# Sums of squares on TensorE, and a first pair's products with the memory's k tiles between them, in a hybrid decoder step

## The chip, the cores and the metric

One core of one Trainium2 chip runs the whole program. The metric is the time of one execution on the device in microseconds (us); the time before is the median of three runs. One further execution was recorded by the profiler; all durations of single instructions are from that one. The engines are TensorE (PE, with its weight loads as PEld), VectorE (DVE), ScalarE (ACT), GpSimd (POOL) and SyncE (SP), whose queue issues all the loads and stores. Every engine takes its own instructions strictly in the order that was fixed when the program was built.

## What is computed

One layer of a decoder step over 1,024 prompt tokens and 8 x 4 sample tokens, model width 2,048, in fp32. Cut to what matters here:

```python
def mixer_layer(x, mem_k, mem_v, ...):
    hn = rmsnorm(x, g_norm)
    proj = hn @ w_in                     # 5904 columns, split among the groups
    ...                                  # A: gated short conv, B: GLA, C: sliding window
    q = rmsnorm(m_q.reshape(b, L, MEM_HEADS, MEM_HD), g_mem_q)
    s = jnp.einsum('blhd,bmhd->bhlm', q, mem_k) * (MEM_HD ** -0.5)
    o_mem = jnp.einsum('bhlm,bmhd->blhd', jax.nn.softmax(s, axis=-1), mem_v)
    ...
    return x + mix @ w_out

def memory_kv(mem, g_mem, w_mem_kv, g_mem_k):        # 256 memory tokens
    kv = rmsnorm(mem, g_mem) @ w_mem_kv              # 2048 x 1024
    k, v = jnp.split(kv, 2, axis=-1)
    return rmsnorm(k.reshape(b, m, MEM_HEADS, MEM_HD), g_mem_k), v.reshape(...)
```

## The kernel before

Features lie on the 128 partitions, the 1,056 tokens (1,024 + 32) along the free axis; `H` is half of them (528), `CG` a quarter (264), `CW` a third (352). A k tile is 128 of the 2,048 features, so there are 16. An fp32 product is made of three TensorE passes: each operand is split into a rounded part h (cast by ACT) and the rest l (subtraction by DVE), and hh, lh and hl are added.

The program runs in stages:

1. **First two** (`first_two`, L380 to L417). Two projection tiles, Dq0 and Dq1, are computed from all 16 k tiles of x times the gain, without the row norm, while x is loaded (`load_x`, L274). ACT squares each k tile (L289) and DVE adds the squares up (L294). At the end `row_norms` (L321) sums over the features on TensorE, forms the reciprocal roots on DVE in small steps (L261 to L270), spreads them over the partitions by transposes (L337) and copies them to `R` (L340, L342). Six evacuations (L417) multiply the two tiles by R. The first 8 k tiles of x stay in SBUF as four blocks B11, B12, B21, B22 (`x0raw`, tiles `xb`).
2. **Memory** (`memory`, L814). 16 k tiles of memory tokens against `w_mem`: 32 weight pieces of 128 x 512, two per k tile, 6 matmuls each (L865). A piece is loaded (`load_piece`, L349), cast by ACT (L364) and subtracted by DVE (L368); odd pieces go to tiles named t, even ones to wh and wl. Between the k tiles runs the generator `first_strands`, which prepares the token operands of the next stage: it normalises the blocks in place (L443), takes a low-rank gate product of them (`rank`, L485), combines the blocks (L458, L459, L464, L473) and splits the seven operands (L431 on ACT, L432 on DVE). What is left of the generator runs after the last k tile.
3. **Pairs** (`first_pair`, L670). 24 pairs of projection tiles; each pair multiplies its weights with the 2 x 2 blocks of x by seven products, in the order B11, T2, B21, T1, T3, B22, T4, 24 matmuls each (`product`, L635, matmuls at L650). This is done for the first 8 k tiles and, by `second_pair`, for the other 8, and then again for the output projection. It is the bulk of the run. Beside each half product one step of a queue of generators (`pipe`) runs: here `memory_out` and the cross-attention heads `d_head`.

Memory pieces and the pairs' weight pieces come from one pool of six buffers, `wr`. A pair has four pieces, (0,0), (1,0), (1,1) and (0,1); those of the first pair are requested ahead of the memory, and `make_weights`, called by `product`, makes the seven weight sets of a pair one by one and requests the next pair's pieces:

```python
wr = self.wp.tile([P, 512], F32, name=self.name("wr"), tag="wr", bufs=6)     # load_piece
t = self.wp.tile([P, 512], F32, name=self.name("wr"), tag="wr", bufs=6)      # load_weights
...
if i == 0:                                                                   # make_weights
    self.load_weights(n + 1, ((0, 0), (1, 0)))
    x = r(0, 0)
elif i == 1:
    v.tensor_tensor(s1, r(1, 0), r(1, 1), op=ALU.add)
    v.tensor_tensor(s2, s1, r(0, 0), op=ALU.subtract)
...
elif i == 4:
    x = r(1, 0)
    v.tensor_tensor(x, r(0, 0), x, op=ALU.subtract)
```

A buffer is free for the next request when the last instruction that reads its piece is done: for a memory piece that is the subtraction at L368; for (0,0) of a pair the difference of set 4, which may be taken early; for (1,0), (0,1) and (1,1) the sets 4, 5 and 6, that is the fifth, sixth and seventh product.

Of the kernel before, what the change touches and what calls it, by code (L numbers as in the profile page):

```python
# [14 lines left out]
P = 128  # L15
# [107 lines left out]
class _Step:  # L123
# [149 lines left out]
    def load_x(self):  # L273
# [3 lines left out]
        self.acc = [None] * 2  # L277
# [8 lines left out]
        def square(k, parts):  # L286
# [33 lines left out]

    def row_norms(self, spare):  # L321

        nc = self.nc
        acc = self.acc[0]
        nc.vector.tensor_tensor(acc, acc, self.acc[1], op=ALU.add)
        for sums in self.token_sums(acc[:, 0:SEQ]):
            pass
        nc.tensor.matmul(spare[:, 0:2], acc[:, TOK - P : TOK], self.ones[:, 0:2], start=True,
                         stop=True)
        r = self.small(NB + 1, tag="rx")  # L330
        self.rsqrt(r[:, 0:NB], sums, 1.0 / D_MODEL, EPS, NB)
        self.rsqrt(r[:, NB : NB + 1], spare[:, 0:1], 1.0 / D_MODEL, EPS, 1)
        for g in range(3):
            ps = self.ps() if g == 1 else spare
            blocks = list(range(4 * g, min(4 * g + 4, NB + 1)))
            for i, n in enumerate(blocks):
                nc.tensor.transpose(ps[:, i * P : i * P + P],  # L337
                                    r[:, n : n + 1].to_broadcast([P, P]), self.ident)
            if g < 2:
                nc.scalar.copy(self.R[:, 512 * g : 512 * g + 512], ps)  # L340
            else:
                nc.scalar.copy(self.R[:, SEQ:TOK], ps[:, P - NS : P])  # L342
# [43 lines left out]
    def first_two(self, evacs):  # L386

        nc = self.nc
        a, b = self.two(), self.two()
# [7 lines left out]
        for kq in range(4):  # L397
            w = [self.take(1) for _ in range(2)]
            for kk in range(4):
# [11 lines left out]
                if kq == 3 and kk == 1:  # L411
                    self.row_norms(b[:, 512:1024])
        for i in range(2):
            dst = evacs[i]
            for c in range(NCH):
                cs = slice(c * CW, c * CW + CW)
                nc.vector.tensor_tensor(dst[:, cs], ps[i][c][:, 0:CW], self.R[:, cs], op=ALU.mult)  # L417

# [15 lines left out]
    def first_strands(self):  # L434
# [5 lines left out]
        for k in range(8):  # L440
            for i in range(2):
# [3 lines left out]
            if k % 2:  # L445
                yield
# [1456 lines left out]
```

## Time and profile before

| | us |
|---|---|
| median of 3 runs | 1579.18 (1578.06 to 1580.34) |
| the profiled execution | 1580.26 |
| its span on the core | 1578.5 |
| PE busy in the span | 1531.3 (97%) |
| DVE busy | 1105.2 (70%) |
| ACT busy | 775.0 (49%) |

The span is from the first to the last instruction; the profiled execution's own time is 1.8 us more. A row of a profile's timeline gives start and duration in us, engine, line, operation, written tile <- read tiles, shapes, count, and in brackets how long the engine had been idle and what ended that. A row of grouped instructions gives, behind the bar, busy time in us and the mean of one in ns, and then the idle time just ahead of them. Matmuls are pipelined: the distance of two starts is what one costs, not the duration shown. Granted clock is the share of full speed that TensorE had.

### The profile page before, as it was taken

What the parts mean: (1) busy time and instruction counts of PE and PEld (TensorE: products, weight loads), DVE (VectorE), ACT (ScalarE), POOL (GpSimd) and SP (SyncE); (2) the same over time, 40 slices, a digit from 0 to 9 for tenths busy, and PEclk for the clock granted to TensorE, in tenths of its full rate; (3) what the DMA queues carried; (4) which work ended last, traced back from release to release, by engine and by line L of the source; (5) the groups of instructions that cost most, each with busy time, mean ns of one, the idle gap of its engine ahead of it and who ended that gap; (6) DMA issues with size and microseconds to landing.
All of it is one profiled execution on the core that took longest, in us unless ns stands there. A gap on an engine that the chain in (4) does not pass through costs nothing.

```text
span 1578.5 us, 30825 instructions
## 1 busy us (share of the span) xinstructions
PE 1531.3 (97%) x12194; PEld 1453.0 (92%) x12194; DVE 1105.2 (70%) x2280; ACT 775.0 (49%) x1622; POOL 23.3 (1%) x35
## 2 busy tenths in 40 slices
PE   8878999999999999999999999999999999999998
PEld 7646999999999999988998888999989999999998
DVE  8998455577555559566767776769779767596664
ACT  8565733222333326563458766445457444263332
POOL 3000000000000000000000000000000000000000
PEclk9999999999999999999999999999999999999999
DMA  7433123266332347358423244245537324587651
GB/s 272 144 107 114 67 101 109 103 244 241 109 108 103 109 144 279 104 126 302 144 84 83 97 88 122 94 134 140 176 111 245 109 96 152 201 285 276 210 204 63
DMA packets 104756, 236.79 MB, mean 150 GB/s; under 512 B 16804, under 2 KB 22820, under 8 KB 104612
## 3 DMA queue, kind: packets, MB, share of 16 engines
q1 hardware_dynamic: 104612, 234.82, 44.7%
q8 instruction: 96, 1.57, 0.4%
q14 instruction: 48, 0.39, 0.1%
HBM read 165.38 MB, written 69.41 MB: 149 GB/s over the span
## 4 chain that ended last, share of the span: by engine, by line
PE 79%; DVE 9%; DMA 5%; ACT 4%; issue 2%; SPq 0%; DVEq 0%; ACTq 0%
PE pj L650 68%; DMA x<-in_xT 2%; DVE wl L632 1%; DMA wr<-in_w_mem 1%; PE ms L865 1%; DVE s L432 1%; PE ms L1224 1%; PE ms L972 1%; PE ms L1002 1%; PE ms L1278 1%; PE ms L1266 1%; DMA sx<-xs 1%; DVE xhl L311 1%; DMA kcd<-in_cache_swa_kT 1%; ACT xhl L310 1%
## 5 line engine op out<-in xcount | busy, mean ns | idle before, releaser
L650 PE MATMUL pj<-s,wh 128*128 128x264 f32 x6720 | 1274.9, 288 | 9.5 <-ACT pj L733 9.0
L650 PEld LDWEIGHTS pj<-s,wh 128*128 128x128 f32 x6720 | 1054.5, 189 | 34.1 <-issue 15.7
L650 PE MATMUL pj<-s,wl 128*128 128x264 f32 x3360 | 957.3, 285 | 0.0
L650 PEld LDWEIGHTS pj<-s,wl 128*128 128x128 f32 x3360 | 634.8, 189 | 3.9 <-issue 3.4
L631 ACT CAST wh<-wr 128x512 fp32r<-128x512 f32 x300 | 186.5, 622 | 252.3 <-PE pj L650 230.6
L632 DVE TENSOR_TENSOR wl<-wr,wh 128x512 fp32r<-128x512 f32 x300 | 206.6, 689 | 112.6 <-ACT wh L631 108.4
L680 DVE TENSOR_TENSOR d<-d,pj 128x528 f32<-128x528 f32 x180 | 121.4, 701 | 112.8 <-PE pj L650 65.6
L631 ACT CAST wh<-ws 128x512 fp32r<-128x512 f32 x120 | 74.5, 621 | 106.8 <-PE pj L650 100.4
L632 DVE TENSOR_TENSOR wl<-ws,wh 128x512 fp32r<-128x512 f32 x120 | 82.7, 689 | 7.0 <-ACT wh L631 6.5
L733 ACT COPY pj<-d 128x528 f32<-128x528 f32 x120 | 72.5, 604 | 16.6 <-DVE u L743 7.3
L432 DVE TENSOR_TENSOR s<-sx,s 128x1056 fp32r<-128x1056 f32 x42 | 51.7, 1254 | 1.8 <-ACT s L431 1.6
L431 ACT CAST s<-sx 128x1056 fp32r<-128x1056 f32 x42 | 44.3, 1079 | 9.9 <-DMA sx<-xs 5.1
L683 ACT COPY d<-pj 128x528 f32<-128x528 f32 x30 | 18.0, 600 | 61.0 <-PE pj L650 61.0
L754 DVE TENSOR_TENSOR d<-d,pj 128x528 f32<-128x528 f32 x30 | 21.1, 704 | 35.7 <-PE pj L650 35.7
L757 DVE TENSOR_TENSOR d<-u,pj 128x528 f32<-128x528 f32 x30 | 21.1, 704 | 34.1 <-PE pj L650 34.0
L689 ACT COPY d<-pj 128x528 f32<-128x528 f32 x30 | 18.0, 601 | 52.2 <-PE pj L650 52.2
L613 DVE TENSOR_TENSOR ws<-wr,wr 128x512 f32<-128x512 f32 x60 | 41.3, 689 | 1.6 <-DMA wr<-in_w_in 0.5
L627 DVE TENSOR_TENSOR wr<-wr,ws 128x512 f32<-128x512 f32 x60 | 41.3, 689 | 1.1
L623 DVE TENSOR_TENSOR wr<-wr,wr 128x512 f32<-128x512 f32 x60 | 41.3, 689 | 1.0
L614 DVE TENSOR_TENSOR ws<-ws,wr 128x512 f32<-128x512 f32 x60 | 41.3, 689 | 1.0
L700 ACT COPY d<-pj 128x528 f32<-128x528 f32 x30 | 18.0, 600 | 47.7 <-PE pj L650 47.7
L696 ACT COPY d<-pj 128x528 f32<-128x528 f32 x30 | 18.0, 600 | 47.1 <-PE pj L650 47.1
(365 smaller groups left out, 1545.2 us busy)
## 6 DMA issues: line engine op xcount, KB each, us to landing
wr<-in_w_in SPq DMA_DIRECT2D x184, 256.0 KB
half_in<-d SPq DMA_DIRECT2D x44, 528.0 KB
d<-half_in SPq DMA_DIRECT2D x44, 528.0 KB
sx<-xs SPq DMA_DIRECT2D x42, 528.0 KB
wr<-in_w_out SPq DMA_DIRECT2D x64, 256.0 KB
x<-in_xT SPq DMA_DIRECT2D x24, 528.0 KB
xs<-t SPq DMA_DIRECT2D x36, 264.0 KB
half_out<-d SPq DMA_DIRECT2D x16, 528.0 KB
```

Source lines behind the costliest of these rows:

```text
L431: nc.scalar.copy(h[:, s], x)
L432: nc.vector.tensor_tensor(l[:, s], x, h[:, s].bitcast(F32), op=ALU.subtract)
L613: v.tensor_tensor(s1, r(1, 0), r(1, 1), op=ALU.add)
L614: v.tensor_tensor(s2, s1, r(0, 0), op=ALU.subtract)
L623: v.tensor_tensor(x, r(0, 0), x, op=ALU.subtract)
L627: v.tensor_tensor(x, x, self.wsum[n][1], op=ALU.subtract)
L631: nc.scalar.copy(wh, x)
L632: v.tensor_tensor(wl, x, wh.bitcast(F32), op=ALU.subtract)
L650: nc.tensor.matmul(ps[:, 512 * c : 512 * c + CG], w[:, ks], x[:, xs], start=(first and kk == 0 and n == 0), stop=(kk == 3 and n == 2), ski ...
L680: nc.vector.tensor_tensor(o, o, bank(ps), op=op)
L733: nc.scalar.copy(bank(ps), x)
L754: tt(ws, zs, bank(w), op=ALU.add)
```

## The change

Three things are changed.

First, the squares. DVE adds nothing; each k tile's squares go to TensorE as they are, in `sum_squares`: four matmuls against a matrix of ones, each 32 columns wide at its own place, accumulate a quarter of the tokens each in a PSUM tile `sums` over all k. Those of the last three k tiles stand behind the main matmuls of k tile 13, and `row_norms` is now a generator whose three parts run beside k tiles 13, 14 and 15. `R` and the two evacuation tiles are requested later.

Second, the order of memory and first pair. `memory` is a generator too, and is not run by itself any more: `product` runs a step of `first_strands` and one k tile of the memory in turn as long as its token operand isn't ready, and `first_strands` runs what is left of the memory ahead of T4. The strands are made in another order, block by block, B11 first. While an operand is missing, `product` makes no weight sets ahead. The masks and the first two heads come behind the first pair.

Third, the memory's tokens are loaded by two transfers of 8 k tiles, and their squares are added in halves.

```diff
@@ load_x @@
-            i = int(k % 4 == 3)
-            if self.acc[i] is None:
-                self.acc[i] = sq
-            else:
-                nc.vector.tensor_tensor(self.acc[i], self.acc[i], sq, op=ALU.add)
+            self.sq[k] = sq
@@ sum_squares, row_norms @@
+    def sum_squares(self, k):
+        for j in range(4):
+            self.nc.tensor.matmul(self.sums[32 * j : 32 * j + 32, 0:CG], self.ones[:, 0:32],
+                                  self.sq[k][:, CG * j : CG * j + CG], start=(k == 0),
+                                  stop=(k == KT - 1), tile_position=(0, 32 * j))
+        self.sq[k] = None
     def row_norms(self, spare):
-        acc = self.acc[0]
-        nc.vector.tensor_tensor(acc, acc, self.acc[1], op=ALU.add)
...
+        rows = self.t5()[:, 0:CG]
+        nc.scalar.copy(rows, self.sums[:, 0:CG])
+        yield
...
+        self.rsqrt(r, t[:, 0:2], 1.0 / D_MODEL, EPS, 8)
+        self.rsqrt(r8[0:8, :], t[0:8, 2], 1.0 / D_MODEL, EPS, 4)
+        yield
+        for j in range(4):
...
+            nc.scalar.copy(self.R[:, CG * j : CG * j + CG], ps[:, 0:CG])
+        yield
@@ first_two @@
-                if kq == 3 and kk == 1:
-                    self.row_norms(b[:, 512:1024])
+                self.sum_squares(k)
+                if k == KT - 3:
+                    for i in (1, 2):
+                        self.sum_squares(k + i)
+                    self.R = self.rtile("R")
+                    norms = self.row_norms(b[:, 512:1024])
+                if k >= KT - 3:
+                    next(norms)
...
@@ first_strands @@
+        normal(0)
+        yield
+        self.split(B11, b11)
+        yield
+        normal(1)
...
+        ranks(range(4))
+        normal(3)
+        yield
+        self.split(B22, b22)
...
+        self.split(T2, b11)
+        yield
+        self.split(B21, b21)
...
+        self.split(T1, b12)
+        yield
+        self.split(T3, b22)
+        yield
+        for _ in self.mem:
+            pass
         self.split(T4, t4)
+        yield
@@ product @@
-        while len(self.wready) <= min(self.wdone + 2, 7 * len(self.pairs) - 1):
+        ahead = 0 if None in self.S else 2
+        while len(self.wready) <= min(self.wdone + ahead, 7 * len(self.pairs) - 1):
             self.make_weights()
+        while self.S[i] is None:
+            next(self.first)
+            next(self.mem, None)
@@ memory @@
             mh, ml = parts[k]
-            next(between, None)
             for c in range(2):
                 wh, wl = self.take(2)
...
-        for _ in between:
-            pass
+            yield
@@ run @@
-                self.memory(pool, self.first_strands())
-                self.masks()
-                for h in range(2):
-                    self.d_head(q[h], h)
+                self.mem, self.first, self.mem_done = self.memory(pool), self.first_strands(), []
                 for n, two in enumerate(self.two_in):
...
                     self.first_pair(self.keep(self.kept(two)))
+                    if n == 0:
+                        self.masks()
+                        for h in range(2):
+                            self.d_head(q[h], h)
```

In the rows below, line numbers of the change are those of the changed file: L636 is the request in `load_weights` (L599 before), L359 that in `load_piece` (L349), L378 the subtraction of a piece (L368), L468 the normalising of a block (L443), L454 the subtraction of a token operand (L432), L691 a product's matmul (L650) and L904 the memory's (L865).

SP's queue at the end of the first stage, before: requests of pieces in the six `wr` buffers, four for the first pair (`in_w_in`), then the memory's third piece and those behind it (`in_w_mem`).

```order
L599 DMA wr86_709<-in_w_in 128x512
L599 DMA wr87_711<-in_w_in 128x512
L599 DMA wr88_713<-in_w_in 128x512
L599 DMA wr89_715<-in_w_in 128x512
L349 DMA wr100_743<-in_w_mem 128x512
L439 DMA t599_737<-in_w_ga 128x256
L349 DMA wr103_749<-in_w_mem 128x512
L349 DMA wr106_761<-in_w_mem 128x512
```

The same place after the change:

```order
L636 DMA wr85_757<-in_w_in 128x512
L636 DMA wr86_759<-in_w_in 128x512
L636 DMA wr87_761<-in_w_in 128x512
L889 DMA mr101_788<-in_memT 128x8x256
L889 DMA mr102_790<-in_memT 128x8x256
L636 DMA wr88_763<-in_w_in 128x512
L636 DMA wr92_768<-in_w_in 128x512
L636 DMA wr93_770<-in_w_in 128x512
L461 DMA t596_776<-in_w_ga 128x256
L359 DMA wr107_804<-in_w_mem 128x512
L359 DMA wr110_810<-in_w_mem 128x512
L359 DMA wr113_822<-in_w_mem 128x512
```

Two pieces of the second pair (wr92 and wr93) now stand between the first pair's four and the memory's third piece, wr107, and the memory's tokens (mr) are ahead of them.

DVE in the memory stage, before: weight subtractions (t and wl from a piece wr) with the normalising of blocks xb between them.

```order
L368 TENSOR_TENSOR wl_817<-wr_789,wh_816 128x512
L368 TENSOR_TENSOR t_829<-wr_814,t_828 128x512
L443 SCALAR_TENSOR_TENSOR xb_130<-xb_130,consts,R_118 128x528
L443 SCALAR_TENSOR_TENSOR xb_132<-xb_132,consts,R_118 128x528
L443 SCALAR_TENSOR_TENSOR xb_130<-xb_130,consts,R_118 128x528
L443 SCALAR_TENSOR_TENSOR xb_132<-xb_132,consts,R_118 128x528
L368 TENSOR_TENSOR wl_845<-wr_826,wh_844 128x512
L837 SCALAR_TENSOR_TENSOR r_867<-mr_801,consts,r_866 128x256 x2
```

After, between two of the early pieces (from the sixth on, wr_838):

```order
L378 TENSOR_TENSOR t_853<-wr_838,t_852 128x512
L468 SCALAR_TENSOR_TENSOR xb_130<-xb_130,consts,R_653 128x528
L454 TENSOR_TENSOR s_975<-xb_129,s_974 128x1056
L468 SCALAR_TENSOR_TENSOR xb_128<-xb_128,consts,R_653 128x528
L454 TENSOR_TENSOR s_975<-xb_130,s_974 128x1056
L378 TENSOR_TENSOR wl_909<-wr_850,wh_908 128x512
L468 SCALAR_TENSOR_TENSOR xb_128<-xb_128,consts,R_653 128x528 x3
L494 TENSOR_TENSOR xb_129<-xb_129,xb_127 128x1056
L494 TENSOR_TENSOR xb_130<-xb_130,xb_127 128x1056
L378 TENSOR_TENSOR t_921<-wr_906,t_920 128x512
```

And after, from the thirteenth piece (wr_998) on:

```order
L378 TENSOR_TENSOR wl_1017<-wr_998,wh_1016 128x512
L378 TENSOR_TENSOR t_1029<-wr_1014,t_1028 128x512
L378 TENSOR_TENSOR wl_1075<-wr_1026,wh_1074 128x512
L378 TENSOR_TENSOR t_1087<-wr_1072,t_1086 128x512
L872 SCALAR_TENSOR_TENSOR r_1128<-mr_790,consts,r_1127 128x256 x2
L378 TENSOR_TENSOR wl_1102<-wr_1084,wh_1101 128x512
L378 TENSOR_TENSOR t_1114<-wr_1099,t_1113 128x512
L378 TENSOR_TENSOR wl_1136<-wr_1111,wh_1135 128x512
```

Early pieces have four to six wide operations on blocks between two weight subtractions, normalising and splitting mixed; from the thirteenth piece on little but the pieces' own subtractions and the memory tokens' (r from mr) is left.

PE at the end of the memory, before: the last piece's matmuls (ms) and then the first product (pj) in one run.

```order
L865 MATMUL ms_720<-t_1240,r_1164 128x512
L865 MATMUL ms_722<-t_1240,r_1164 128x512
L865 MATMUL ms_720<-t_1241,r_1164 128x512
L865 MATMUL ms_720<-t_1240,r_1165 128x512
L865 MATMUL ms_722<-t_1241,r_1164 128x512
L865 MATMUL ms_722<-t_1240,r_1165 128x512
L650 MATMUL pj_1307<-s_976,wl_1314 128x264
L650 MATMUL pj_1307<-s_977,wh_1313 128x264
L650 MATMUL pj_1307<-s_976,wh_1313 128x264
```

After, in the second product, T2 (s_1123 and s_1124 are the two parts of its operand, r_900 and r_901 the two parts of the memory's fifth and sixth k tile):

```order
L904 MATMUL ms_786<-wh_952,r_901 128x512
L691 MATMUL pj_767<-s_1123,wh_891 128x264
L691 MATMUL pj_767<-s_1123,wl_892 128x264
L904 MATMUL ms_785<-t_964,r_900 128x512
L904 MATMUL ms_787<-t_964,r_900 128x512
L904 MATMUL ms_785<-t_965,r_900 128x512
L904 MATMUL ms_785<-t_964,r_901 128x512
L904 MATMUL ms_787<-t_965,r_900 128x512
L904 MATMUL ms_787<-t_964,r_901 128x512
L691 MATMUL pj_767<-s_1124,wh_891 128x264
L691 MATMUL pj_767<-s_1123,wh_891 128x264
L691 MATMUL pj_767<-s_1123,wl_892 128x264
```

The products' matmuls now stand between the memory's, from its third k tile to its last one, and each waits in PE's order for the pieces ahead of it.

More of the change, by code (lines that the diff above doesn't have):

```diff
@@ L326, in row_norms @@
-        for sums in self.token_sums(acc[:, 0:SEQ]):
-            pass
[L328 to L342, printed above, removed]
+        rows = self.t5()[:, 0:CG]
@@ new lines, in row_norms @@
+        nc.scalar.copy(rows, self.sums[:, 0:CG])
+        yield
+        for x in range(2):
+            nc.tensor.transpose(spare[:, x * P : x * P + P], rows[:, x * P : x * P + P],
+                                self.ident)
+        nc.tensor.transpose(spare[0:8, 2 * P : 3 * P], rows[:, 2 * P : CG], self.ident)
+        t = spare[:, 0 : 3 * P].rearrange("p (x j c) -> p x j c", x=3, j=4)[:, :, :, 0]
+        r, r8 = self.small(8, tag="rx"), self.small(4, tag="rx8")
+        self.rsqrt(r, t[:, 0:2], 1.0 / D_MODEL, EPS, 8)
@@ new lines, in row_norms @@
+        self.rsqrt(r8[0:8, :], t[0:8, 2], 1.0 / D_MODEL, EPS, 4)
+        yield
+        for j in range(4):
+            ps = spare if j % 2 else self.sums
+            for x in range(2):
+                nc.tensor.transpose(ps[:, x * P : x * P + P],
+                                    r[:, 4 * x + j : 4 * x + j + 1].to_broadcast([P, P]),
+                                    self.ident)
+            nc.tensor.transpose(ps[:, 2 * P : CG], r8[0:8, j : j + 1].to_broadcast([8, P]),
+                                self.ident[0:8, 0:8])
+            nc.scalar.copy(self.R[:, CG * j : CG * j + CG], ps[:, 0:CG])
@@ L384, in take, with first_two @@
         return self.ready[p]
-    def first_two(self, evacs):
+    def first_two(self):
         nc = self.nc
+        self.sums = self.ps()
         a, b = self.two(), self.two()
@@ L417, in first_two @@
                 nc.vector.tensor_tensor(dst[:, cs], ps[i][c][:, 0:CW], self.R[:, cs], op=ALU.mult)
+        self.sums = None
+        return evacs
     def split(self, i, src, half=None):
@@ L811, in gate, with memory @@
         return lambda *z: self.pipe.now(work(*z))
-    def memory(self, pool, between):
+    def memory(self, pool):
         nc, I, O = self.nc, self.I, self.O
@@ L842, in squares @@
             nonlocal acc
[L843 removed]
+            t = raw[k][:, 0 : 8 * N_MEM]
             nc.scalar.activation(t, t, AF.Square)
[L845 to L851 removed]
+            for w in (4 * N_MEM, 2 * N_MEM, N_MEM):
+                nc.vector.tensor_tensor(t[:, 0:w], t[:, 0:w], t[:, w : 2 * w], op=ALU.add)
+            if k:
+                nc.vector.tensor_tensor(acc, acc, t[:, 0:N_MEM], op=ALU.add)
+            else:
+                acc = self.hp.tile([P, H], F32, name=self.name("acc"), tag="u", bufs=1)[:, 0:N_MEM]
+                nc.vector.tensor_copy(acc, t[:, 0:N_MEM])
+        for k in range(2):
+            raw[k] = self.stile(F32, "mr")
+            nc.sync.dma_start(out=raw[k][:, 0 : 8 * N_MEM].rearrange("p (k t) -> p k t", k=8),
+                              in_=I["memT"][8 * k : 8 * k + 8].rearrange("k p t -> p k t"))
         prepare(0)
@@ L855, in memory @@
                 prepare(k + 2)
-            if k % 4 == 2:
-                squares(k // 4)
+            if k % 8 == 6:
+                squares(k // 8)
+                raw[k // 8] = None
             mh, ml = parts[k]
-            next(between, None)
             for c in range(2):
```

60 lines of the change are left out of this document (21 added, 39 removed).

## The prediction

> **What bounds the kernel now.** I read the page's first part, then busy times by stretch, then the chain of waits where TensorE is not full. Over the whole span TensorE (PE) is the limit; the second fence gives, for six stretches of 20 us, length, busy time of PE, PEld, DVE, ACT and POOL, granted TensorE clock, DMA share and GB/s.
>
> ```profile
> PE 1531.3 (97%) x12194; PEld 1453.0 (92%) x12194; DVE 1105.2 (70%) x2280; ACT 775.0 (49%) x1622; POOL 23.3 (1%) x35
> ```
>
> ```profile
> 60.00:80.00 20.00, 17.21 (x83) 11.60 (x84) 17.83 (x36) 9.04 (x16) 0.00 (x0) 0.91 0.50 159
> 80.00:100.00 20.00, 16.10 (x88) 9.17 (x87) 18.89 (x22) 13.58 (x21) 0.00 (x0) 1.00 0.31 103
> 100.00:120.00 20.00, 14.99 (x51) 9.53 (x50) 19.82 (x23) 14.14 (x18) 0.00 (x0) 0.91 0.36 108
> 120.00:140.00 20.00, 15.62 (x65) 10.66 (x64) 16.12 (x34) 10.55 (x21) 1.05 (x5) 1.00 0.38 124
> 140.00:160.00 20.00, 18.98 (x151) 17.71 (x150) 14.84 (x60) 12.66 (x36) 0.00 (x0) 1.00 0.35 110
> 160.00:180.00 20.00, 20.00 (x146) 18.49 (x145) 12.98 (x38) 14.59 (x39) 0.00 (x0) 1.00 0.19 70
> ```
>
> PE has gaps until about 146 us and none after; between 60 and 140 us VectorE (DVE) is nearly full. So the time is set by how late PE becomes full and by the PE work then left. Two rows of the chain give the point and the price of a product's matmul: 60.94/502 = 0.121 us. The two groups below are the first pair's matmuls that ran before 146 us: 27 + 14 = 41 of 7 x 24 = 168.
>
> ```profile
> 146.06 3.77 PE pj L650 x31
> ...
> 199.08 60.94 PE pj L650 x502
> ```
>
> ```profile
> L650 PE MATMUL pj<-s,wh 128*128 128x264 f32 x27 | 5.1, 287 | 0.0
> L650 PE MATMUL pj<-s,wl 128*128 128x264 f32 x14 | 4.1, 289 | 0.0
> ```
>
> Without the cross-attention heads, which both kernels do beside full products, the second pair would start at 146.06 + 127 x 0.121 = 161.5 us. **That is the mark**: the change wins or loses what its second pair starts earlier or later.
>
> In the memory stage each of 32 weight pieces of `w_mem` is loaded into a buffer `wr`, cast by ScalarE (ACT), subtracted by DVE, and only then is its buffer free for the next load. The chain of waits shows one such turn, and the loads' queue waits for the subtraction (total us, times, longest):
>
> ```profile
> 91.05 2.66 DMA wr<-in_w_mem
> ...
> 93.73 0.63 ACT t L364
> ...
> 94.39 0.69 DVE t L368
> ...
> 104.63 3.32 DMA wr<-in_w_mem
> ...
> 109.35 2.87 DMA wr<-in_w_mem
> ```
>
> ```profile
> SPq L349 <- DVE wl L368: 36.1, 13, 8.2
> ...
> SPq L349 <- DVE t L368: 8.4, 12, 2.3
> ```
>
> A turn without a queue is 2.66 + 0.63 + 0.69 and gaps, 4.05 us. With DVE's queue it was longer: the odd pieces' subtractions run from 72.25 to 137.61 us, 13 turns of 5.03 us.
>
> ```profile
> 72.25 0.69 DVE L368 TENSOR_TENSOR t<-wr,t 128x512 fp32r<-128x512 f32 x1
> ...
> 137.61 0.69 DVE L368 TENSOR_TENSOR t<-wr,t 128x512 fp32r<-128x512 f32 x1
> ```
>
> **The buffers, the part that decides.** There are six `wr` buffers. Before, the first pair's four pieces hold four of them through the whole memory stage, so memory pieces go through the other two, and two turns run side by side: two pieces per 5 us. After, the first pair's first weights are made ahead of most of the memory, and `make_weights` at its first step loads two pieces of the second pair (SP's rows in the section on the change have them ahead of the memory's third piece). Only piece (0, 0) of the first pair has been given back by then: its sums are formed early. So 3 + 2 = 5 buffers are held and **one** is left, until the fifth product's weights (T3, piece (1, 0)) are made. The memory's first two pieces are loaded earlier; the next 22 go through one buffer, one after the other; the last 8 go through two. That is 22 + 4 = 26 turns in series, where before 15 pairs of turns sufficed.
>
> **The first stage.** Removed: DVE's additions of squares and the trailing norms. Added: 16 x 4 fp32 matmuls of 32 columns on PE. The rows give 18 main matmuls in 43.73 - 40.83 = 2.90 us, and four such sums of 256 tokens in 55.64 - 55.08 = 0.56, so 0.58 at 264.
>
> ```profile
> 12.55 0.32 PE L408 MATMUL pj<-xhl,wh 128*128 128x352 f32 x1
> ...
> 40.83 1.62 PE L408 MATMUL ms<-xhl,r 128*128 128x352 f32 x9
> ...
> 43.73 1.62 PE L408 MATMUL ms<-xhl,r 128*128 128x352 f32 x9
> ...
> 55.08 0.64 PE L937 MATMUL ms<-sq,ones 128*32 128x256 f32 x8 [0.24 <-DVE sq L325]
> 55.64 0.38 PE L328 MATMUL pj<-ones,sq 128*128 128x2 f32 x2
> ...
> 63.23 0.32 PE L408 MATMUL pj<-xhl,wh 128*128 128x352 f32 x1
> ```
>
> PE is already the pace there, so the sums are not hidden. Main matmuls end at 12.55 + 15 x 2.90 + 16 x 0.58 = 65.3 us, where the row above has the last three groups from 62.3 to 63.5. Bounds of the sums: nothing, if they fit into PE's small waits, to 16 x 0.64 = 10.2; I take 9.3, the value of the nearest row. The additions saved on DVE give nothing once PE sets the pace. The last three sums stand ahead of the last two k tiles, so the norms' sums and reciprocal roots lie under 36 main matmuls; after them come the spreading of the norms over R, the six evacuations and the first block.
>
> ```profile
> L443 DVE SCALAR_TENSOR_TENSOR xb<-xb,consts,R 128x528 f32<-128x528 f32 x16 | 11.2, 764 | 0.0
> L368 DVE TENSOR_TENSOR t<-wr,t 128x512 fp32r<-128x512 f32 x15 | 10.3, 689 | 0.7 <-ACT t L364 0.5
> ...
> L417 DVE TENSOR_TENSOR dq<-pj,R 128x352 f32<-128x352 f32 x3 | 1.5, 525 | 0.1
> ```
>
> ```profile
> 60.39 0.65 PE L337 MATMUL pj<-ident,sm 128*128 128x128 f32 x4 [1.30 <-DVE sm L270]
> ...
> 61.70 1.01 DVE L417 TENSOR_TENSOR dq<-pj,R 128x352 f32<-128x352 f32 x2
> ```
>
> From 65.3 us: from the norms' transposes to the first evacuation 1.3, as between these two rows; six evacuations at 0.5, 3.0; four normalisings at 11.2/16 = 0.70, 2.8; one weight subtraction 0.7. The fourth memory piece is ready at about **73 us**.
>
> **From 73 us, nine turns paced by DVE.** Between the fourth and the thirteenth subtraction DVE's order holds the normalising, combining and splitting of blocks, from these rows and the two of L443 and L368 above:
>
> ```profile
> L432 DVE TENSOR_TENSOR s<-xb,s 128x2112 fp32r<-128x2112 f32 x4 | 9.3, 2352 | 0.0
> ...
> L837 DVE SCALAR_TENSOR_TENSOR r<-mr,consts,r 128x256 fp32r<-128x256 f32 x16 | 7.1, 480 | 1.5 <-ACT r L836 1.5
> ...
> L432 DVE TENSOR_TENSOR s<-xb,s 128x1056 fp32r<-128x1056 f32 x4 | 4.9, 1252 | 0.0
> L848 DVE TENSOR_TENSOR mr<-mr,mr 128x1024 f32<-128x1024 f32 x3 | 3.7, 1220 | 0.0
> ...
> L458 DVE TENSOR_TENSOR xb<-xb,xb 128x1056 f32<-128x1056 f32 x2 | 2.4, 1253 | 0.0
> ```
>
> Twelve normalisings 8.4, four wide and four half splits 9.3 + 4.9, combinations 4 x 2.4 = 9.6, six memory parts 2.7, ten weight subtractions 6.9, halvings of the memory's squares and one evacuation some 3.3 (the 1024 wide one 1.2, the others narrower): 45 us, less some 0.05 of overlap in each of 45 instructions: **43 to 44 us**, to 117 us. These turns would take 9 x 4.05 = 36 by the chain alone, so the buffer costs little here.
>
> **Then eleven turns paced by the one buffer.** DVE has little left and waits for each piece: 11 x 4.05 = **44.6 us**, to 162 us. I take the shortest load, 2.66, since with one buffer no second load of `w_mem` is in flight to slow it; the bounds are that and the 5.03 of the turns before. Products two to five run on PE meanwhile, hidden.
>
> **Last four turns, two buffers.** ACT squares the memory's second half there (2048 wide, twice the 1.06 of a 1024 wide one in the row below), and DVE adds it and splits T4: some 4.6 us a turn, 18.5, to 180.5 us. Then four matmuls and the rest of T4: 1.5 us. The second pair starts at **182 us** against 161.5.
>
> ```profile
> L844 ACT ACTIVATE mr<-mr 128x1024 f32<-128x1024 f32 x4 | 4.2, 1062 | 2.8 <-DVE r L837 2.7
> ```
>
> ```profile
> 145.43 0.63 PE L906 MATMUL ms<-ident,t 128*128 128x128 f32 x4 [1.02 <-DVE sm L270]
> ```
>
> **Sum.** The memory's first key transposes, 0.6 us in this row and ahead of 146.06 before, now come after the second pair's start. 182 + 0.6 - 161.5 = +21 us on the profiled execution (1580.26 us: span 1578.5 and 1.8 around it), 1601 us; against the median of 1579.18 it is about 1600. I forecast **1601 us**. Masks, mask POOL work and the heads' chains move beside pairs two and three, where PE is full (20.00 of 20) and ACT and DVE have room; without that cover they cost waits like the 1.02 us of that row.
>
> A rule against the trace: TensorE's clock. At 114 to 118 us the granted clock fell to 0.57 though PE's waits since 105 us had been 1.3 us at most (stretch, then timeline).
>
> ```profile
> 114.00:118.00 4.00, 3.48 (x8) 2.61 (x9) 4.00 (x6) 1.45 (x2) 0.00 (x0) 0.57 0.42 131
> ```
>
> ```profile
> 107.57 0.73 PE L865 MATMUL ms<-wh,r 128*128 128x512 f32 x2 [1.33 <-ACT wh L364]
> ```
>
> The Trainium skill, TensorE: Matmul & The Clock Gate, "What's actually happening", has the clock halved after an idle window of about 3.4 us. By it turns of 4.05 us with six matmuls in each would keep the clock, and the sum stays 1601; by the row sparse work is enough to lose it, the six matmuls still fit into a turn, and the second pair would begin slow, for some 2 us more, 1603.
>
> **Rivals.**
> - *Every turn as long as before.* Nothing but the number in series changes, and queues on ACT and DVE stretch each of the 24 turns after 73 us to 5.03: 73 + 121 + 1.5 = 195, 1615 us. For it: the 13 turns measured. Against: DVE is nearly idle after 117 us.
> - *Faster: DVE is the bound, not the buffer.* If two buffers still served the memory, DVE's work (the same sum as before, started 2 to 3 us later) would end near 143 us, with most products done beside it; the second pair starts at 145: 161.5 - 145.6 = 16 us gained, 1564 us. It decides if at most four buffers are held when the third memory piece is loaded. For it: 19.82 of 20 on DVE. Against: the count of buffers.
>   The Trainium skill, Perfetto Trace Analysis, "Optimization Strategy", says that interleaving regimes with different contended engines may improve performance; by that rule this rival would come true, and the trace agrees as to the two regimes (rows at 100 and 160 us).
> - *The sums cost nothing.* PE hides them in waits and overlap, everything after is 9 us earlier: 1592 us. For it: each of the four is 32 columns wide where a main matmul has 128. Against: the 0.56 us of the L937 row already has the four together.
> - *No change.* Short turns throughout and the heads' waits saved cancel the loss: 1580; it needs turns of 3.2 us, below any row.
>
> **How the numbers follow.** Forecast 0.64; long turns 0.18; free sums 0.08; faster 0.06; no change 0.04. The low end adds free sums and short first turns (DVE sum 40): 1588. The high end takes long turns and 5 us of waits in the DVE stage: 1620. Faster by over 0.2% (what a measurement here can tell from no change) 0.06, within it 0.04, slower 0.90.
>
> **What would show it.** In the profile after: ACT's casts waiting for loads of `w_mem`, 2 to 3 us before nearly each, from about 117 to 160 us; no two such loads in flight there; PE full only from about 182 us; sums of squares at about 0.58 us per k tile; DVE's busy share under half after 117 us. Loads in pairs, or PE full before 150 us, would make the prediction wrong.

## The result and the profile after

The changed kernel takes 1607.72 us (median of 4 runs, 1607.12 to 1609.01) against 1579.76 us beside it: ratio 1.0173, 95% interval 1.0159 to 1.0186, **28 us slower**. The forecast was 1601 us with a range from 1588 to 1620.

The page's first line after, and then the stretches of 20 us as they were shown of before (length, busy time of PE, PEld, DVE, ACT, POOL, granted TensorE clock, DMA share, GB/s):

```profile
PE 1553.4 (97%) x12316; PEld 1462.6 (91%) x12316; DVE 1084.8 (68%) x2268; ACT 773.5 (48%) x1621; POOL 19.0 (1%) x35
```

```profile
60.00:80.00 20.00, 18.93 (x131) 13.93 (x130) 14.48 (x45) 8.23 (x15) 0.00 (x0) 1.00 0.13 40
80.00:100.00 20.00, 14.39 (x88) 7.63 (x86) 20.00 (x27) 9.03 (x15) 0.00 (x0) 0.94 0.16 53
100.00:120.00 20.00, 14.01 (x47) 10.01 (x48) 18.59 (x20) 13.18 (x14) 0.00 (x0) 0.67 0.17 54
120.00:140.00 20.00, 14.75 (x32) 8.91 (x32) 4.46 (x8) 3.89 (x7) 0.00 (x0) 0.53 0.21 66
140.00:160.00 20.00, 15.25 (x78) 12.41 (x76) 6.44 (x11) 5.80 (x11) 0.00 (x0) 0.91 0.20 66
160.00:180.00 20.00, 18.18 (x92) 15.12 (x92) 13.06 (x22) 10.19 (x16) 0.00 (x0) 0.91 0.38 120
180.00:200.00 20.00, 19.61 (x146) 18.59 (x145) 18.27 (x63) 11.09 (x31) 1.08 (x5) 1.00 0.50 173
```

Where DVE was nearly full before, from 60 to 140 us, it is full only until 120, and then no engine is: between 120 and 140 us PE counts 14.75 us with 32 matmuls, most of it at half clock, DVE 4.46, ACT 3.89, and the DMA engines move 66 GB/s where they moved 124. They wait for one another around one buffer. The chain of waits shows that ring (start, duration, what; only issuing, 0.02 us each, lies between these rows):

```profile
120.42 2.58 DMA wr<-in_w_mem
123.02 0.63 ACT t L374
123.67 0.70 DVE t L378
124.39 2.49 DMA wr<-in_w_mem
126.91 0.63 ACT wh L374
127.56 0.70 DVE wl L378
```

A piece is loaded, cast, subtracted, and only then the next load starts (at 124.39 us, where the subtraction ends at 124.37). Before, such a load started while the other buffer's piece was still worked on. The timeline of DVE gives the pace; in brackets the time that DVE was idle before, and what ended it:

```profile
75.65 0.68 DVE L378 TENSOR_TENSOR t<-wr,t 128x512 fp32r<-128x512 f32 x1
...
119.70 0.69 DVE L378 TENSOR_TENSOR wl<-wr,wh 128x512 fp32r<-128x512 f32 x1 [0.34 <-ACT wh L374]
123.67 0.69 DVE L378 TENSOR_TENSOR t<-wr,t 128x512 fp32r<-128x512 f32 x1 [3.28 <-ACT t L374]
127.56 0.69 DVE L378 TENSOR_TENSOR wl<-wr,wh 128x512 fp32r<-128x512 f32 x1 [3.19 <-ACT wh L374]
...
155.43 0.69 DVE L378 TENSOR_TENSOR t<-wr,t 128x512 fp32r<-128x512 f32 x1 [2.61 <-ACT t L374]
161.31 0.69 DVE L378 TENSOR_TENSOR wl<-wr,wh 128x512 fp32r<-128x512 f32 x1 [5.19 <-ACT wh L374]
...
166.25 0.69 DVE L378 TENSOR_TENSOR t<-wr,t 128x512 fp32r<-128x512 f32 x1 [3.65 <-ACT t L374]
...
184.80 0.69 DVE L378 TENSOR_TENSOR t<-wr,t 128x512 fp32r<-128x512 f32 x1
```

These are the 4th, the 13th to 15th, the 22nd to 24th and the last of the 32 pieces. Until the 13th, DVE's own work stands between them. From there on nine turns take 3.9 to 4.1 us, and DVE sits idle for some 3 of them in the rows shown. Two of the eleven turns are longer (161.31 - 155.43 = 5.88 and 166.25 - 161.31 = 4.94). The second pair's first matmul is the 169th of the products and stands second in this row of PE's timeline, at 187.4 us, against a mark of 161.5:

```profile
187.33 0.40 PE L691 MATMUL pj<-s,wh 128*128 128x264 f32 x2
```

### The profile page after: what moved, and what is told of

Its sections match the earlier page's. It is cut to its first block, busy times and chain, and to the rows that moved or that the text cites. A ratio compares the mean times of both kernels' runs of the same rounds, so it can differ in the third digit from the quotient of the medians.

```text
span 1606.3 us, 31049 instructions
## 1 busy us (share of the span) xinstructions
PE 1553.4 (97%) x12316; PEld 1462.6 (91%) x12316; DVE 1084.8 (68%) x2268; ACT 773.5 (48%) x1621; POOL 19.0 (1%) x35
## 4 chain that ended last, share of the span: by engine, by line
PE 80%; DVE 9%; DMA 5%; ACT 3%; issue 2%; SPq 0%; ACTq 0%; DVEq 0%
PE pj L691 66%; PE pj L419 2%; DVE s L454 2%; PE ms L419 2%; DMA wr<-in_w_mem 1%; DVE wl L669 1%; DMA sx<-xs 1%; DMA x<-in_xT 1%; PE ms L1261 1%; PE ms L1315 1%; PE ms L904 1%; PE ms L1039 1%; PE ms L1303 1%; DMA kcd<-in_cache_swa_kT 1%; DVE xb L468 1%
## 5 line engine op out<-in xcount | busy, mean ns | idle before, releaser
L691 PE MATMUL pj<-s,wh 128*128 128x264 f32 x6720 | 1278.5, 288 | 11.8 <-ACT pj L774 9.9
L691 PEld LDWEIGHTS pj<-s,wh 128*128 128x128 f32 x6720 | 1057.4, 189 | 40.0 <-issue 15.5
L691 PE MATMUL pj<-s,wl 128*128 128x264 f32 x3360 | 958.3, 285 | 0.0
L691 PEld LDWEIGHTS pj<-s,wl 128*128 128x128 f32 x3360 | 636.5, 189 | 4.3 <-issue 3.4
L454 DVE TENSOR_TENSOR s<-sx,s 128x1056 fp32r<-128x1056 f32 x42 | 51.6, 1251 | 1.4 <-ACT s L453 1.2
L650 DVE TENSOR_TENSOR ws<-wr,wr 128x512 f32<-128x512 f32 x60 | 41.3, 688 | 4.7 <-DMA wr<-in_w_in 3.6
```

The source lines that it names most:

```text
L454: nc.vector.tensor_tensor(l[:, s], x, h[:, s].bitcast(F32), op=ALU.subtract)
L691: nc.tensor.matmul(ps[:, 512 * c : 512 * c + CG], w[:, ks], x[:, xs], start=(first and kk == 0 and n == 0), stop=(kk == 3 and n == 2), ski ...
```

## The experiments

Two questions: is it the count of buffers or the new order of the work that costs 28 us, and what do the sums on TensorE cost? Each run's median stands beside that of the kernel before, taken in the same series on the same chip. The diffs show only what matters here.

| run | us (median, range) | before | ratio, 95% interval |
|---|---|---|---|
| two buffers | 1574.05 (1572.71 to 1575.48) | 1579.68 | 0.9962 (0.9949 to 0.9975) |
| three buffers | 1575.19 (1571.03 to 1577.51) | 1579.68 | 0.9969 (0.9955 to 0.9983) |
| sums on DVE | 1607.60 (1604.75 to 1610.05) | 1579.68 | 1.0176 (1.0157 to 1.0194) |
| two of 16 sums | 1598.43 (1597.88 to 1598.58) | 1579.68 | 1.0118 (1.0103 to 1.0133) |
| before, one buffer | 1652.63 (1647.17 to 1656.45) | 1579.71 | 1.0449 (1.0426 to 1.0472) |
| two buffers, sums in fours | 1570.75 (1569.78 to 1575.48) | 1579.71 | 0.9945 (0.9932 to 0.9957) |
| two buffers, sums on DVE | 1568.85 (1568.16 to 1569.47) | 1579.71 | 0.9928 (0.9916 to 0.9940) |
| two buffers, GpSimd | 1587.79 (1586.01 to 1590.34) | 1579.71 | 1.0048 (1.0036 to 1.0060) |
| two buffers, half the sums each | 1569.23 (1565.39 to 1572.77) | 1580.70 | 0.9923 (0.9906 to 0.9939) |
| three buffers, sums on DVE | 1571.24 (1568.56 to 1573.81) | 1580.70 | 0.9936 (0.9921 to 0.9951) |
| the change again | 1608.12 (1607.02 to 1609.65) | 1579.39 | 1.0181 (1.0167 to 1.0195) |
| sums on DVE again | 1607.28 (1604.65 to 1608.10) | 1579.39 | 1.0168 (1.0154 to 1.0182) |

### Two buffers, and three

One request of the second pair is moved from the first to the sixth step of `make_weights`, for the first pair only:

```diff
 if i == 0:
-    self.load_weights(n + 1, ((0, 0), (1, 0)))
+    self.load_weights(n + 1, ((0, 0), (1, 0)) if n else ((0, 0),))
...
 elif i == 5:
-    self.load_weights(n + 1, ((1, 1), (0, 1)))
+    self.load_weights(n + 1, ((1, 1), (0, 1)) if n else ((1, 0), (1, 1), (0, 1)))
```

For three buffers both are moved there, and (1, 1) and (0, 1) behind the memory:

```diff
 if i == 0:
-    self.load_weights(n + 1, ((0, 0), (1, 0)))
+    if n:
+        self.load_weights(n + 1, ((0, 0), (1, 0)))
...
 elif i == 5:
-    self.load_weights(n + 1, ((1, 1), (0, 1)))
+    self.load_weights(n + 1, ((1, 1), (0, 1)) if n else ((0, 0), (1, 0)))
...
 for _ in self.mem:
     pass
+self.load_weights(1, ((1, 1), (0, 1)))
 self.split(T4, t4)
```

> The changed kernel, but of the second pair's four weight pieces only (0,0) is requested at the first step of make_weights; (1,0) is requested at the sixth and so the memory's pieces have two buffers instead of one. Nothing is left out of the computation. Buffers (my theory): the stretch up to about 120 us stays, since DVE sets its pace; the turns of 4.05 us from there run two by two, and the 19 pieces left then need 38 to 40 us (19 x 2.05, or the 19 x 6 matmuls at 0.23 and 96 products' matmuls at 0.121 us that TensorE has to do meanwhile: 26 + 12). Pair two starts near 164 us instead of 187.5, the time is 1584 to 1588 us. Rival, the order of the work (products between the memory's matmuls, strands and subtractions in one DVE queue) costs the time and not the buffers: 1602 us or more.

> The same with both early requests of the second pair moved to the sixth step of make_weights (the other two behind the memory), so that the memory's pieces have three buffers. Nothing is left out. Buffers: one more buffer gives little, since with two TensorE and DVE already set the pace after 120 us: 1581 to 1587 us, at most 4 us below the run with two buffers. If loads alone set the pace (4.05 us / 3 a piece), 19 pieces take 26 us and the time is near 1572. Rival, the order of the work: 1602 us or more.

One moved request takes 34 us away (1607.72 to 1574.05), and the changed kernel is then 0.38% faster than the one before. The rival, that the new order of the work costs the time and not the buffer, asked for 1602 us or more and did not come. The edit moves a request and no work; but the order in which the built program gives each engine its instructions differs between the two runs too, so that this run alone does not part the one from the other. The ring in the trace of the change, where each load starts as the subtraction before it ends, and the kernel before with one buffer, further down, point to the buffer. A stretch of the run with two buffers, and its last subtraction of a piece:

```profile
120.00:140.00 20.00, 20.00 (x134) 18.42 (x133) 17.05 (x23) 15.87 (x24) 0.00 (x0) 1.00 0.38 119
```

```profile
152.17 0.69 DVE L378 TENSOR_TENSOR t<-wr,t 128x512 fp32r<-128x512 f32 x1 [0.36 <-ACT t L374]
```

This stretch has 134 matmuls where the change had 32, at full clock, and DVE is at 17.05 of 20 where it was at 4.46. The last piece is done at 152.9 instead of 185.5 us, and the second pair starts at 154.8 instead of 187.4. My number for this run, 1584 to 1588, was 10 us too high: I had kept the first stretch as it was in the change, with the 13th piece's subtraction beginning at 119.7 us. With a second buffer it is the 20th that begins at 119.8; on DVE the pieces now stand two by two between the blocks.

The third buffer gave nothing more (1575.19 against 1574.05; the ranges overlap); my 1581 to 1587 was too high again. The memory does end earlier, with its last subtraction beginning at 142.2 us and the second pair at 150.4, but PE then waits 2.87 us in the second pair, by the profile for the cast of a weight set. ACT makes that cast at 158.60 us, behind the memory's output steps (L923 to L928, from 153.49 us on):

```profile
159.25 0.63 PE L945 MATMUL ms<-ident,t 128*128 128x128 f32 x4 [2.87 <-ACT wh L670]
```

### The kernel before with one buffer

```diff
-wr = self.wp.tile([P, 512], F32, name=self.name("wr"), tag="wr", bufs=6)
+wr = self.wp.tile([P, 512], F32, name=self.name("wr"), tag="wr", bufs=5)
...
-t = self.wp.tile([P, 512], F32, name=self.name("wr"), tag="wr", bufs=6)
+t = self.wp.tile([P, 512], F32, name=self.name("wr"), tag="wr", bufs=5)
```

> The kernel before with five wr buffers instead of six, so that its memory pieces have one buffer; order of the work and everything else as before, nothing left out. Buffers: 30 pieces in series at 4.05 us or more from about 60 us on, 122 us, end near 185 us instead of 138; the second pair starts 45 to 50 us later, 1620 to 1635 us, with the granted clock well under 1 in that stretch. Rival, one buffer is harmless as long as products don't stand between the memory's matmuls: within 5 us of before. Five buffers for the pairs later may add some us behind 250 us, which the trace shows apart.

It takes 73 us more. The same picture comes up without any part of the change:

```profile
120.00:140.00 20.00, 10.69 (x26) 5.47 (x24) 4.79 (x7) 4.57 (x8) 0.00 (x0) 0.69 0.22 66
160.00:180.00 20.00, 12.44 (x28) 7.23 (x28) 7.71 (x22) 4.29 (x8) 0.00 (x0) 0.54 0.19 52
```

Again 66 GB/s, and from 120 to 140 us DVE and ACT at under 5 us of 20. The last piece's subtraction begins at 200.8 us (137.6 before). The second pair starts at 231.9 us, 60.6 later than the 171.3 that the same count gives of before; the profiled spans differ by 75.3, so some 15 us come after it, where the pairs too have a buffer less. No run takes these apart. I had guessed 45 to 50 for the first part, without adding DVE's work in the earlier turns. That the change with one buffer loses less has two parts. Its last piece begins 16 us earlier (184.8), since the last eight go through two buffers. And its second pair starts 2.7 us behind that, here 31 us, since the products stand between the pieces there and behind them here.

### The sums of squares

On DVE again, beside the change's other parts (for one buffer and, with the same edit, for two and three):

```diff
-self.sq[k] = sq
+i = int(k % 4 == 3)
+if self.acc[i] is None:
+    self.acc[i] = sq
+else:
+    nc.vector.tensor_tensor(self.acc[i], self.acc[i], sq, op=ALU.add)
...
-self.sum_squares(k)
 if k == KT - 3:
-    for i in (1, 2):
-        self.sum_squares(k + i)
+    nc.vector.tensor_tensor(self.acc[0], self.acc[0], self.acc[1], op=ALU.add)
+    self.sum_squares(k)
```

Two of 16 sums only (this kernel leaves the squares of 14 k tiles out of the norms):

```diff
-for j in range(4):
+for j in range(4 if k in (0, KT - 1) else 0):
     self.nc.tensor.matmul(self.sums[32 * j : 32 * j + 32, 0:CG], self.ones[:, 0:32],
```

> The changed kernel with the squares added up on DVE again, as before, and one group of four sums on TensorE at k tile 13; all else as in the change. Nothing is left out. TensorE paid 16 x 0.77 us for the sums in the trace of the change (0.58 for the four, and 0.19 more in the main matmuls around them), but before it also waited some 6 us for x and DVE there. Sums cost what I think: the main matmuls end 4 to 5 us earlier, and since DVE's work on the first blocks follows them, the time is 1602.5 to 1604 us. Rival, DVE needs the relief: its additions (15 wide ones) delay the splits of x as before, and the time is the same, 1606 to 1609 us.

> The changed kernel with the sums of 14 of the 16 k tiles left out (only those of the first and the last are made), so neither TensorE nor DVE adds the squares. The row norms are then wrong and with them the output. If the sums on TensorE are the whole delay of the first stage, main matmuls end 5 to 8 us earlier (14 x 0.77 = 10.8 less the waits for x that come back), 1599 to 1603 us. If the loads of x set the pace there anyway: 1606 us or more.

> The changed kernel with the sums on DVE, as in the run sums on DVE, more rounds. With two buffers the sums on TensorE cost 5.2 us (1574.1 against 1568.9), with one the medians were level, yet the trace had the memory's last subtraction 2.3 us earlier. If one buffer hides part of the sums' cost: 1603 to 1606 us, that is 2 to 4 us below the change. If the whole of it: level with the change within 1 us.

> The changed kernel itself once more, beside the next one, so that the two are compared within one series: 1606 to 1609 us.

> The run with two buffers, with the squares added up on DVE again as in the kernel before. Nothing is left out. With one buffer the two ways took the same time (1607.6 and 1607.7). If that was so because the first stage costs DVE what it costs TensorE, the same holds here: 1572.5 to 1576 us. If DVE, which is full from 73 to 152 us with two buffers, then pays for each addition: 1577 to 1583.

Without 14 of the sums the time falls by 9.3 us (1607.72 to 1598.43): on TensorE they are not hidden. But with one buffer the same sums on DVE cost as much: 1607.60 and 1607.28 against 1607.72 and 1608.12, ranges that overlap. With two buffers DVE is the cheaper place by 5.2 us (1568.85 against 1574.05; the ranges are apart, and so are the intervals of the ratios), and the second pair starts 5.0 us earlier there (149.8 against 154.8). My expectation for one buffer failed, and the one for two, level, as well. The traces show where the gain goes with one buffer. The first block is normalised 7 us earlier with sums on DVE; the first row is of the change, the others are of the first run with sums on DVE:

```profile
72.93 2.79 DVE L468 SCALAR_TENSOR_TENSOR xb<-xb,consts,R 128x528 f32<-128x528 f32 x4
```

```profile
65.97 2.79 DVE L468 SCALAR_TENSOR_TENSOR xb<-xb,consts,R 128x528 f32<-128x528 f32 x4
...
69.28 2.12 DVE L468 SCALAR_TENSOR_TENSOR xb<-xb,consts,R 128x528 f32<-128x528 f32 x3
71.32 2.35 DVE L454 TENSOR_TENSOR s<-xb,s 128x2112 fp32r<-128x2112 f32 x1
73.59 0.68 DVE L381 TENSOR_TENSOR t<-wr,t 128x512 fp32r<-128x512 f32 x1
```

The fourth piece, though, is subtracted only 2 us earlier there (73.59, the last of these rows, against 75.65). In the change it follows the first four normalisings; with sums on DVE the third piece, three more normalisings and a wide split come between, 4.9 us from 68.68 to 73.59. So the order that DVE was given eats 5 of the 7 us. It is not that one buffer can't take a lead: with 14 sums left out the 13th piece begins at 110.22 us instead of 119.70, and the second pair starts 10.5 us earlier. With sums on DVE the second pair starts 2.4 us earlier in the first trace and no earlier in the second, whose 13th piece begins at 120.40. What another order on DVE would give was not tried.

The halves of the load were tried with two buffers. Sums of four k tiles made together:

```diff
-self.sum_squares(k)
+for i in range(4 if k % 4 == 3 and k < KT - 3 else 0):
+    self.sum_squares(k - 3 + i)
 if k == KT - 3:
-    for i in (1, 2):
-        self.sum_squares(k + i)
+    for i in range(12, KT):
+        self.sum_squares(i)
```

Two k tiles' squares added on DVE, then summed on TensorE:

```diff
 self.sq[k] = sq
+if k % 2:
+    nc.vector.tensor_tensor(sq, sq, self.sq[k - 1], op=ALU.add)
...
-self.sum_squares(k)
+if k % 2 and k < KT - 1:
+    self.sum_squares(k)
 if k == KT - 3:
-    for i in (1, 2):
-        self.sum_squares(k + i)
+    self.sum_squares(KT - 1)
```

> The run with two buffers (one request of the second pair moved), with the sums of squares of four k tiles made together instead of one by one: 4 places in TensorE's order instead of 14 where 32 column sums stand between main matmuls. Nothing is left out. In the trace of the change a k tile's 18 main matmuls took 3.09 us beside the sums and 2.90 without. If the change of the matmul's shape costs these 0.19 us, 10 places less save 1.9 us: 1571.5 to 1573 us. Rival, the 0.19 us have another cause (each matmul a little slower): 1573 to 1575.5, no difference.

> The run with two buffers, with the squares of two k tiles added on DVE (8 additions instead of 15 or none) and 8 groups of sums on TensorE instead of 16. Nothing is left out. From 12 to 60 us TensorE is full with all sums on it (48.0 of 48 us) and DVE with all additions on it (47.7 of 48). If these two set the pace in turn, the half of each leaves both some room: the main matmuls end at 60 to 63 us, against 68.5 with all sums on TensorE and some 60 with all on DVE; the norms come sooner behind them than with all on DVE: 1565 to 1570 us, at least level with sums on DVE (1568.9). Rival, sums cost what they cost wherever they stand: halfway between 1574.1 and 1568.9, 1570.5 to 1572.5.

> The run with three buffers (both early requests of the second pair moved), with the squares added up on DVE. Nothing is left out. With the sums on TensorE a third buffer changed nothing that can be told (1575.2 against 1574.1), since DVE sets the pace of the stage from two buffers on. The same here: 1567 to 1571 us. Rival, the third buffer pays as soon as the stage starts earlier: under 1566.

The rows of PE's timeline show what a place in the order costs. First the change, then the run with sums in fours:

```profile
40.71 1.61 PE L419 MATMUL ms<-xhl,r 128*128 128x352 f32 x9
42.26 0.66 PE L321 MATMUL ms<-xr,ones 128*32 128x264 f32 x8
...
44.38 1.61 PE L419 MATMUL ms<-xhl,r 128*128 128x352 f32 x9
```

```profile
45.05 1.62 PE L419 MATMUL ms<-xhl,r 128*128 128x352 f32 x9
47.95 1.61 PE L419 MATMUL ms<-xhl,r 128*128 128x352 f32 x9
49.50 1.99 PE L321 MATMUL ms<-xr,ones 128*32 128x264 f32 x32
...
52.96 1.62 PE L419 MATMUL ms<-xhl,r 128*128 128x352 f32 x9
```

A k tile with its sums takes 44.38 - 40.71 = 3.67 us, one without 47.95 - 45.05 = 2.90; so the sums cost 0.77, not 0.58. Four together cost 52.96 - 47.95 - 2.90 = 2.11, which is 0.53 each. If a k tile's four sums cost s and a place between main matmuls e, then s + e = 0.77 and 4 s + e = 2.11: s is 0.45 and e 0.32 us. Ten places less are then worth 3.2 us, where my expectation had 1.9; the main matmuls end 2.8 us earlier (65.7 instead of 68.5), and the median fell by 3.3. The ranges of the two runs still overlap, so the trace carries this reading rather than the time.

Half on each engine ends level with all on DVE (1569.23 against 1568.85). One row of each run says why little is left to gain there, from 12 to 60 us: with two buffers and all sums on TensorE, all on DVE, and half on each.

```profile
12.00:60.00 48.00, 48.00 (x340) 39.58 (x339) 25.65 (x35) 37.37 (x66) 8.04 (x6) 1.00 0.75 252
```

```profile
12.00:60.00 48.00, 46.05 (x286) 44.35 (x285) 47.74 (x63) 39.33 (x68) 12.30 (x6) 1.00 0.74 248
```

```profile
12.00:60.00 48.00, 48.00 (x328) 43.24 (x327) 37.81 (x48) 38.09 (x68) 8.73 (x6) 1.00 0.74 256
```

TensorE is at 46.05 of 48 even with the sums on DVE. The third buffer beside sums on DVE gives nothing either (1571.24, at the upper end of what was expected).

### GpSimd's share

```diff
-eng = nc.gpsimd if 0 < n < 8 else nc.vector
+eng = nc.gpsimd if 0 < n < 8 or n > 8 and n % 4 == 3 else nc.vector
...
-    nc.vector.tensor_tensor(t[:, 0:w], t[:, 0:w], t[:, w : 2 * w], op=ALU.add)
+    nc.gpsimd.tensor_tensor(t[:, 0:w], t[:, 0:w], t[:, w : 2 * w], op=ALU.add)
...
-    nc.vector.tensor_tensor(acc, acc, t[:, 0:N_MEM], op=ALU.add)
+    nc.gpsimd.tensor_tensor(acc, acc, t[:, 0:N_MEM], op=ALU.add)
```

> The run with two buffers, with work taken from DVE: GpSimd adds the memory tokens' squares in halves (six additions, 4.6 us on DVE) and makes every fourth weight piece's subtraction of the memory stage (8 x 0.69 us = 5.5). Nothing is left out. If DVE sets the end of that stage (74.0 of 79 us busy from 73 to 152 us), the second pair starts up to 10 us earlier, less what GpSimd's slower subtraction (1.3 us) holds a buffer longer, 8 x 0.65: 1565 to 1571 us. Rival, TensorE (71.8 of 79) and the two buffers already set it: 1572 to 1576. Rival, GpSimd and DVE slow each other: over 1576.

It loses 13.7 us against the same kernel without it, where I had expected 3 to 9 us of gain; the rival that the two engines slow each other came true. The groups by line of the run with GpSimd, and then of the run with two buffers:

```profile
L468 DVE SCALAR_TENSOR_TENSOR xb<-xb,consts,R 128x528 f32<-128x528 f32 x16 | 17.0, 1116 | 0.0
L378 POOL TENSOR_TENSOR t<-wr,t 128x512 fp32r<-128x512 f32 x8 | 15.9, 1991 | 79.7 <-ACT t L374 79.7
```

```profile
L468 DVE SCALAR_TENSOR_TENSOR xb<-xb,consts,R 128x528 f32<-128x528 f32 x16 | 11.3, 760 | 0.0
```

The same 16 normalisings take 17.0 us instead of 11.3, and a subtraction on GpSimd 1.99 us where 1.30 was assumed. The timeline of the run with GpSimd shows the two beside each other; the first and the last row are single instructions that start together:

```profile
95.21 2.37 POOL L881 TENSOR_TENSOR mr<-mr 128x1024 f32<-128x1024 f32 x1 [0.48 <-ACT mr L879]
```

```profile
93.48 7.51 DVE L468 SCALAR_TENSOR_TENSOR xb<-xb,consts,R 128x528 f32<-128x528 f32 x4
```

```profile
95.21 2.93 DVE L468 SCALAR_TENSOR_TENSOR xb<-xb,consts,R 128x528 f32<-128x528 f32 x1
```

While GpSimd works, four normalisings take 7.51 us instead of 2.79. The one at 95.21 ends 0.56 us behind GpSimd's addition (98.14 against 97.58), and each of the three others in that row ends 0.56 or 0.57 us behind the GpSimd instruction beside it. Eleven of the 16 keep their 0.75 or 0.76 us, five take 1.23 to 2.93. GpSimd's eight subtractions take 1.30 to 3.85 us. The second pair starts at 168.5 us, 13.7 later, so the whole loss lies ahead of it. How it divides between DVE's slowing and buffers held longer by GpSimd was not tried.

## Why the prediction was right, step by step

The mechanism came as forecast: five buffers held, 22 pieces through one, ACT's casts waiting for each load, TensorE full from about 187 us on. The run with two buffers shows it from the side of the change, the run with five buffers from the side of the kernel before. The rival that it was the order of the work finds no support in either. No term of the sum came out shorter than forecast, so the hit does not rest on errors that cancel.

The terms of the sum:

- **First stage, the mis-sized one.** Main matmuls were to end at 65.3 us; they ended at 68.5. The sums were put at 16 x 0.58 = 9.3 us. Measured are thirteen k tiles at 0.77 us and the last three, which stand together, at 62.09 - 57.52 - 2.90 = 1.67, some 11.7 in all: each place between main matmuls costs 0.32 us beside the sums themselves. The norms' transposes add 65.35 - 62.09 - 2.90 = 0.4; the remaining 0.4 I did not trace. The fourth piece was ready at 75.65 + 0.68 = 76.3 instead of 73.
- **Nine turns paced by DVE.** Forecast 44 us, measured 76.3 to 120.4, 44.1.
- **Eleven turns of one buffer.** Forecast 44.6 us, measured 120.4 to 166.9, 46.5. Nine took the 3.9 to 4.1 us of the chain. In the turn of 5.88 us the cast was due at some 158.7 us, as far behind the cast before it as in the other turns, and came 2 us later. On ACT it stood behind a copy of a product that PE had not finished until 159.2, and behind a head's squares, about 1 us each. In the prediction heads cost nothing, as their cover was looked for in pairs two and three:

```profile
159.22 0.60 ACT L737 COPY d<-pj 128x528 f32<-128x528 f32 x1 [3.82 <-PE pj L691]
159.71 1.06 ACT L964 ACTIVATE sq<-dq 128x1024 f32<-128x1024 f32 x1
160.67 0.61 ACT L374 CAST wh<-wr 128x512 fp32r<-128x512 f32 x1
```

In the turn of 4.94 us a second load of `w_mem` was in flight (issued at 162.63 us, 0.60 behind the first), and the cast began 3.57 us after its load's issue, where the chain shown above has 2.5 to 2.6.

- **Last eight pieces and T4.** Forecast 20, measured 166.9 to 187.4, 20.5.
- **The mark.** 187.4 + 0.6 - 161.5 = 26.5 us; the spans differ by 1606.3 - 1578.5 = 27.8. So the second pair's start carries nearly all of the loss, with 1.3 us from elsewhere that I did not trace.

The rivals. Turns of 5.03 us throughout (1615) did not come: the shortest load held in nine turns of eleven, and the one with a second load beside it took 4.94. Free sums (1592) did not come: leaving them out saves 9.3 us. The faster rival, by its own condition of four held buffers, is what the run with two buffers made, and the sign is right: 5.6 us faster than before, where it had been priced at 16. Its price took DVE's work to start 2 to 3 us later than before; the first block is normalised at 73.67 us in that run, where the first row of before is this:

```profile
64.52 2.12 DVE L443 SCALAR_TENSOR_TENSOR xb<-xb,consts,R 128x528 f32<-128x528 f32 x3
```

That is 9 us. With the sums on DVE the first block comes at 67.85, 3.3 us later than before, and the gain is 10.9 us; the other 5 us of the price stay open. By the Trainium skill, Perfetto Trace Analysis, "Optimization Strategy", regimes with different contended engines may gain from being interleaved; the runs agree once a second buffer is there (0.9962, and 0.9928 with the sums on DVE), and disagree with one buffer (1.0173).

The clock. It was 0.67 between 100 and 120 us and 0.53 between 120 and 140. The waits of PE in the latter stretch of the change (total us, times, longest):

```profile
PE ms L904 <- ACT wh L374: 4.3, 3, 2.2
PE ms L904 <- ACT t L374: 3.2, 3, 1.2
```

No wait is longer than 2.2 us, and none from 60 to 120 us is either. By the Trainium skill, TensorE: Matmul & The Clock Gate, "What's actually happening", which asks for an idle window of about 3.4 us, the clock would have been kept, if that means 3.4 us without any matmul; this trace disagrees, and the measurement decides. What share of work is enough to keep the clock no run here shows. It cost no time inside the turns, as the prediction had it; and the second pair began at full clock (1.00 from 180 to 200 us), so the 2 us that the prediction had for a slow start did not come. These rows are of the change, the first two from a stretch at nearly full clock (0.96 from 111 to 116 us) and the others from the slow one:

```profile
112.45 0.39 PE L904 MATMUL ms<-wl,r 128*128 128x512 f32 x1
112.68 0.39 PE L904 MATMUL ms<-wh,r 128*128 128x512 f32 x1
...
128.60 0.63 PE L904 MATMUL ms<-wl,r 128*128 128x512 f32 x1
129.03 0.63 PE L904 MATMUL ms<-wh,r 128*128 128x512 f32 x1
```

A matmul is 0.43 us behind the last instead of 0.23, but six of them still fit into a turn of 4 us.

## What to carry to other kernels

Before work is moved ahead, count who holds the buffers of each shared pool at the place it moves to: a request made early holds its buffer until its reader runs, and a stream left with one buffer pays load, cast and subtraction in series, 4 us a piece here instead of two pieces in 5. The cure can be one request: moving it turned 28 us of loss into a gain of 5.6. And work taken from one full engine to another is a gain only if the other has room in that very stage: TensorE had some 2 of 48 us, so with two buffers the sums were better left on DVE, with which the change becomes 0.7% faster than the kernel before.

## What had not been expected of the hardware

- Four sums of 32 columns cost 0.77 us between main matmuls of 128 columns and 0.53 when sixteen stand together. By these two figures a place among the main matmuls costs 0.32 us, whether four sums stand there or sixteen; the twelve that stand together in the change (1.67 us) fit that.
- DVE's normalisings took half as long again on average (0.760 to 1.116 us) when GpSimd worked on SBUF beside some of them, and GpSimd's subtraction 1.99 us instead of 1.30. The Trainium skill, SBUF — State Buffer, "SBUF: two separate sides", has the two engines share a pair of ports that one of them holds for a whole instruction; the run agrees: four normalisings in a row each ended 0.56 to 0.57 us behind the GpSimd instruction beside it. The rows from 12 to 60 us above show it the other way round: GpSimd's six subtractions there are busy for 8.04 us with the sums on TensorE and for 12.30 with DVE adding.
- The clock falls in sparse work, with no wait of TensorE longer than 2.2 us here (0.53) and 2.7 in the kernel before with one buffer (0.54 from 160 to 180 us).
